# Sums of weights made ahead: seven more pairs a layer with seven products in the down projections of a two-layer mixer kernel

## The chip, the cores and the metric

The kernel runs on one core of a Trainium2 chip. TensorE (PE) multiplies matrices; VectorE (DVE), ScalarE (ACT) and GpSimd (POOL) work on tiles in the on-chip memory, SBUF; PE's results gather in eight banks of PSUM. SyncE (SP) and POOL issue the transfers (DMAs), each through a queue of its own, and 16 DMA engines carry them out. The metric is the device time of one execution in microseconds, the median of several runs. One execution is also taken with the hardware profiler; it has a time of its own, and all durations here come from it.

## The reference, cut to what matters

The model has two layers, on 256 positions of width 2048, in float32. Each layer is a token mixer and a gated MLP with a convolution of width 3:

```python
def conv_ffn(x, w_up, conv_w, conv_b, w_down):
    h = x @ w_up                                  # 256x2048 @ 2048x11008
    C = h.shape[-1]
    h = lax.conv_general_dilated(h, conv_w[:, None, :], ...) + conv_b
    a, g = jnp.split(h, 2, axis=-1)
    return (jax.nn.silu(g) * a) @ w_down          # 256x5504 @ 5504x2048

for i in range(DEPTH):                            # DEPTH = 2
    m = gmlp_mixer(...) if i % 2 == 0 else mla_mixer(...)
    x = layer_norm(ALPHA * x + m, ...)
    x = layer_norm(ALPHA * x + conv_ffn(x, ...), ...)
```

The change concerns `conv_ffn` in both layers: `x @ w_up` is the up projection, `@ w_down` the down projection.

## The kernel before, in words

**Precision.** Each operand of a matmul is split into a high part (a rounded copy, which ACT makes: CAST) and a low part (what the copy lost, which VectorE makes: a subtraction). A product then takes three matmuls: high by high, high by low, low by high. Weights come from memory in float32 as `raw` tiles of 128 x 2048 and are split to `wh` and `wl`.

**Pairs.** The 5504 rows of `w_down` are 43 blocks of 128, taken in 22 pairs (the last holds a single block), and the 2048 columns in two halves of 1024. A pair of blocks with half the columns and the two blocks of 128 positions is a product of 2 by 2 blocks. The eight-product way ("wide") does it in 8 products, 24 matmuls of 128 x 512. The seven-product way is Winograd's: 7 products, 21 matmuls, but it needs sums of weights (`ts`, split to `th` and `tl`) and sums of activations (turned ones, `dn..sx` or `dn..px`) beside the plain parts. Of the plain weights it needs three quarters, 1536 of 2048 columns.

**Kinds.** `PLAN` says for each pair of both halves how it is done: `e` wide; `s` seven with the sums made on the spot by `_seven` (three additions on VectorE, two more splits); `p` parked, a seven whose parts `wh`, `wl`, `th`, `tl` were all made earlier. A layer has 25 `e` (two of them the single block), 10 `s` and 9 `p`.

**Parking.** The parts of the `p` pairs are made while the up projection runs. `park_all` is a generator of small jobs; at set points of the up projection's loop, `next(jobs, None)` takes one. For each pair POOL's queue fetches the weights (`ask`, tile `praw`), one job splits the plain part, the next makes the sums in place (four additions of 512 columns on VectorE) and asks for the next pair, the third splits the sums. The four parts, 3.5 MB a pair, are stored to DRAM through POOL's queue and come back (`fetch`, tiles `fwh`, `fwl`, `fth`, `ftl`) through the same queue a few pairs ahead of their use.

**Order and room.** The feed (class `Feed`) loads and splits ahead of PE by counts: `next()` has two more chunks split than are used and two more loaded beyond these (fewer at a half's end). Tiles are slots of pools: 3 of `raw`, 14 of `big` (the split parts and the activations' parts), 6 of `side` (parked parts). An instruction that writes a tile waits for its slot: SP's next load waits until VectorE has split the chunk that held the slot, and a split waits until PE has used the one that held its tiles. On each engine instructions run in the written order. In the last layer the last four pairs of the last half are kept open and finished together at the end (`late`, skew 4).

**The up projection** takes 86 pieces of `w_up` in groups of four (`gi`), 128 x 2048 each; a piece is split in two halves of 1024 columns. Two groups, 8 and 9, are done as one in pairs instead. Job points are places 1 and 2 of groups 2 to 21, save near that one.

In the trace, `up` is the up projection, `upf` its first group, `dn_q`, `dn_p` and `dn_e` are PSUM banks of the down projection, `xhl` the split input.

Of the kernel before, what the change touches and what calls it, by code (L numbers as in the profile page):

```python
# [8 lines left out]
F32 = mybir.dt.float32  # L9
# [6 lines left out]
P = 128  # L16
# [57 lines left out]
KEEP = {"wide": 4, "seven": 6, "parked": 6}  # L74


def plan(n_k):
# [4 lines left out]
class Feed:  # L82
# [10 lines left out]
    def _load(self):  # L93
        ap, cols, kind = self.chunks[self.loaded][:3]
        if kind == "parked":
            self.fetch(self.loaded)
            self.loaded += 1
            return
        t = self.pool.tile([P, 2048], F32, tag="raw", name=f"raw{self.loaded}", bufs=SLOTS["raw"])
        if len(ap.shape) == 3:  # L100
            self.behind(self.nc.sync.dma_start(t.rearrange("p (k c) -> p k c", k=ap.shape[1]), ap))
        else:
            step = 1024 if self.loaded < 3 else cols
            for o in range(0, cols, step):
                self.behind(self.nc.sync.dma_start(t[:, o : o + step], ap[:, o : o + step]))
        self.raw[self.loaded] = t
        self.loaded += 1

    def _split(self):
        i = self.split  # L110
        cols, kind = self.chunks[i][1:3]
        if kind == "parked":
            self.split += 1
            return
        raw = self.raw.pop(i)
        if kind == "seven":
            self.parts[i] = self._seven(i, raw)
# [18 lines left out]
    def _seven(self, i, raw):  # L136
# [23 lines left out]
    def park(self, i, raw, coming, later):  # L160
# [3 lines left out]
        add = lambda o, a, b: pin(nc.vector.tensor_tensor(o, a, b, ALU.add))  # L164
        self.kept[i] = kept = {}

        def store(n, t, cols):
            d = self.dram.tile([P, cols], F32, tag=f"kept{n}{i}", name=f"kept{n}{i}", bufs=1)
            pin(nc.gpsimd.dma_start(d, t[:, 0:cols].bitcast(F32)))
            kept[n] = d  # L170

        for n, o, cols in (("w", 512, 1536), ("t", 0, 2048)):
            hi, lo = tile(f"p{n}h", F32R), tile(f"p{n}l", F32R)
            pin(nc.scalar.copy(hi[:, 0:cols], raw[:, o : o + cols]))  # L174
            pin(nc.vector.tensor_tensor(lo[:, 0:cols], raw[:, o : o + cols], hi[:, 0:cols].bitcast(F32), ALU.subtract))  # L175
            store(f"{n}h", hi, cols)
            store(f"{n}l", lo, cols)
            if n == "w":
                yield
                r = [raw[:, 512 * i : 512 * (i + 1)] for i in range(4)]  # L180
                add(r[1], r[1], r[0])
                add(r[0], r[0], r[2])
                add(r[2], r[2], r[1])
                add(r[3], r[3], r[2])
                if later is not None:
                    coming.append(self.ask(later))
                yield

    def fetch(self, i):

# [29 lines left out]
def trunk(ctx: ExitStack, tc: tile.TileContext, x, xT, gm_in, gm_wout, ffn_up, ffn_dn,  # L220
# [44 lines left out]
    def back(w, n_k):  # L265

        for hf, units in enumerate(plan(n_k)):
            c = slice(hf * 1024, (hf + 1) * 1024)
            for u, kind in units:
                if 2 * u + 1 == n_k:  # L270
                    chunks.append((w[2 * u, :, c], 1024, kind))
                    continue
                if kind == "parked":
                    parked.append(len(chunks))
                chunks.append((w[2 * u : 2 * u + 2, :, c].rearrange("k p c -> p k c"), 2048, kind))

    def up(layer):

        for gi in range(22):
            if gi - 1 in UP_TOKEN:  # L280
                continue
            if gi not in UP_TOKEN:
                chunks.extend((ffn_up[layer, i], 2048, "") for i in range(4 * gi, min(4 * gi + 4, n_up)))
# [257 lines left out]
    def down(n_k, src, tag, ln, acts, skew=SKEW, tiles=None, beside=None):  # L541
# [6 lines left out]
        for hf, units in enumerate(seq):  # L548
# [3 lines left out]
            for i, (u, kind) in enumerate(units):  # L552
# [11 lines left out]
                if left < skew:  # L564
                    late.append((a, *got))
                elif kind == "wide":
                    acc.eight(a, *got)
                else:
                    acc.seven(a, sums, *got, 512 if kind == "parked" else 0)
# [421 lines left out]
    def ffn(layer, ln, acc, end, last):  # L991
# [75 lines left out]
        for gi in range(1, 22):  # L1067
# [438 lines left out]
```

## Time and profile before

| | us |
|---|---|
| median of 3 runs (lowest, highest) | 2456.43 (2456.2, 2456.98) |
| profiled execution, its own time | 2455.5 |
| its span | 2453.7 |
| PE busy in the span | 2447.7 |
| VectorE busy | 2135.5 |
| ACT busy | 1515.1 |
| up projection of layer 1, from 1972.8 to 2223.0: its main part | 250.2 |
| down projection of layer 1, from 2223.0 to 2444.0 | 221.0 |

How to read it: matmuls are pipelined and their ends are modelled, so a row's mean duration is longer than the distance from one matmul to the next; the pace is a stretch's time by the number of matmuls in it. Line numbers are those of the kernel before; a row names the tile written, the tiles read, the shape and the count. In the views of stretches the columns after the engines' busy times are the granted clock of PE, the DMA engines' share and GB/s.

### The profile page before, as it was taken

What the parts mean: (1) busy time and instruction counts of PE and PEld (TensorE: products, weight loads), DVE (VectorE), ACT (ScalarE), POOL (GpSimd) and SP (SyncE); (2) the same over time, 40 slices, a digit from 0 to 9 for tenths busy, and PEclk for the clock granted to TensorE, in tenths of its full rate; (3) what the DMA queues carried; (4) which work ended last, traced back from release to release, by engine and by line L of the source; (5) the groups of instructions that cost most, each with busy time, mean ns of one, the idle gap of its engine ahead of it and who ended that gap; (6) DMA issues with size and microseconds to landing.
All of it is one profiled execution on the core that took longest, in us unless ns stands there. A gap on an engine that the chain in (4) does not pass through costs nothing. (4 is left out here: it accounts for less than half of the span.)

```text
span 2453.7 us, 32463 instructions
## 1 busy us (share of the span) xinstructions
PE 2447.7 (100%) x12349; PEld 2078.4 (85%) x12349; DVE 2135.5 (87%) x2831; ACT 1515.1 (62%) x2022; POOL 120.4 (5%) x232
## 2 busy tenths in 40 slices
PE   9999999999999999999999999999999999999999
PEld 7888888888888888888888888988888888888887
DVE  7999889989898798988878897868799898878798
ACT  6666777766556666666655466665666666655553
POOL 0000000000000000000001100000001000000100
PEclk9999999999999999999999999999999999999999
DMA  7556665648776687788888985443579687887895
GB/s 293 197 207 214 229 200 192 221 168 308 244 269 245 242 322 287 250 306 335 307 295 321 345 315 178 175 165 122 210 284 341 216 313 305 335 316 274 328 351 195
DMA packets 122508, 639.19 MB, mean 261 GB/s; under 512 B 11096, under 2 KB 11360, under 8 KB 80752
## 3 DMA queue, kind: packets, MB, share of 16 engines
q1 hardware_dynamic: 91632, 460.37, 52.5%
q0 software_dynamic: 30720, 176.75, 19.0%
q8 instruction: 97, 1.59, 0.3%
q14 instruction: 59, 0.48, 0.1%
HBM read 558.38 MB, written 78.69 MB: 260 GB/s over the span
## 5 line engine op out<-in xcount | busy, mean ns | idle before, releaser
L133 DVE TENSOR_TENSOR wl<-raw,wh 128x1024 fp32r<-128x1024 f32 (+4 forms) x625 | 940.5, 1521 | 117.7 <-ACT wh L130 93.3
L130 ACT CAST wh<-raw 128x1024 fp32r<-128x1024 f32 (+4 forms) x625 | 794.1, 1295 | 323.8 <-PE up L240 82.4
L240 PE MATMUL up<-xhl,wh 128*128 128x512 f32 x2368 | 552.2, 390 | 0.0
L240 PEld LDWEIGHTS up<-xhl,wh 128*128 128x128 f32 x2368 | 439.8, 188 | 88.2
L240 PEld LDWEIGHTS up<-xhl,wl 128*128 128x128 f32 x2368 | 294.1, 192 | 5.8
L240 PE MATMUL up<-xhl,wl 128*128 128x256 f32 x2368 | 296.6, 283 | 0.0
L130 ACT CAST th<-ts 128x1536 fp32r<-128x1536 f32 (+1 forms) x172 | 177.4, 1050 | 133.9 <-DVE ts L140 105.0
L133 DVE TENSOR_TENSOR tl<-ts,th 128x1536 fp32r<-128x1536 f32 (+1 forms) x172 | 203.5, 1219 | 20.8 <-PE ub L240 8.2
L240 PE MATMUL ub<-wh,xhl 128*128 128x512 f32 x516 | 161.0, 393 | 0.0
L140 DVE TENSOR_TENSOR ts<-ts,raw 128x512 f32<-128x512 f32 x172 | 118.1, 686 | 1.9
L240 PEld LDWEIGHTS ub<-wh,xhl 128*128 128x128 f32 x516 | 96.9, 188 | 21.8 <-issue 1.9
L140 DVE TENSOR_TENSOR ts<-raw 128x1024 f32<-128x1024 f32 x86 | 104.8, 1218 | 5.1 <-PE ub L240 2.0
L240 PE MATMUL ub<-wl,xhl 128*128 128x512 f32 x258 | 100.5, 389 | 0.0
L240 PE MATMUL v_q<-wh,xhl 128*128 128x512 f32 x224 | 70.7, 391 | 0.0
L240 PE MATMUL v_p<-wh,xhl 128*128 128x512 f32 x192 | 60.0, 389 | 0.0
L240 PEld LDWEIGHTS ub<-wl,xhl 128*128 128x128 f32 x258 | 48.4, 188 | 10.2
L240 PEld LDWEIGHTS v_q<-wh,xhl 128*128 128x128 f32 x224 | 42.0, 188 | 9.9 <-ACT wh L130 1.3
L164 DVE TENSOR_TENSOR praw<-praw 128x512 f32<-128x512 f32 x72 | 49.4, 686 | 0.6
L175 DVE TENSOR_TENSOR ptl<-praw,pth 128x2048 fp32r<-128x2048 f32 x18 | 41.2, 2286 | 3.4 <-ACT pth L174 3.4
L774 ACT ACTIVATE lny<-lnt,lncol 128x128 f32<-128x128 f32 x96 | 36.3, 467 | 12.0 <-PE lnt L770 11.9
L240 PE MATMUL v_q<-wl,xhl 128*128 128x512 f32 x112 | 43.7, 390 | 0.0
L240 PE MATMUL mo<-wh,oT 128*128 128x512 f32 x128 | 42.8, 412 | 0.0
(1910 smaller groups left out, 4656.5 us busy)
## 6 DMA issues: line engine op xcount, KB each, us to landing
raw<-in_ffn_up_dram SPq DMA_DIRECT2D x172, 1024.0 KB, 6.5
raw<-in_gm_in_dram SPq DMA_DIRECT2D x93, 1024.0 KB, 5.4
raw<-in_ffn_dn_dram SPq DMA_DIRECT2D x66, 1024.0 KB, 7.7
raw<-in_gm_wout_dram SPq DMA_DIRECT2D x48, 1024.0 KB, 5.8
praw<-in_ffn_dn_dram POOLq DMA_DIRECT2D x18, 1024.0 KB, 13.7
keptth<-pth POOLq DMA_DIRECT2D x18, 1024.0 KB, 8.2
kepttl<-ptl POOLq DMA_DIRECT2D x18, 1024.0 KB, 9.6
fth<-keptth POOLq DMA_DIRECT2D x18, 1024.0 KB, 9.4
```

Of the source, the lines that this page charges most:

```text
L130: cast = self.nc.scalar.copy(hi, raw)
L133: self.nc.vector.tensor_tensor(lo, raw, hi.bitcast(F32), ALU.subtract)
L140: add = lambda o, a, b: self.nc.vector.tensor_tensor(o, a, b, ALU.add)
L164: add = lambda o, a, b: pin(nc.vector.tensor_tensor(o, a, b, ALU.add))
L175: pin(nc.vector.tensor_tensor(lo[:, 0:cols], raw[:, o : o + cols], hi[:, 0:cols].bitcast(F32), ALU.subtract))
L240: recent[0] = nc.tensor.matmul(o, l, r, start=start, stop=stop, skip_group_check=True)
L774: nc.scalar.activation(y[:, j], t[:, j * P : (j + 1) * P], AF.Identity, bias=lncol[:, o : o + 1], scale=lncol[:, g : g + 1])
```

## The change

A third kind of seven-product pair, `a` ("added"), comes beside the two. Of such a pair only the sums are made ahead: in the up projection POOL's queue fetches the weights, one job makes the four additions in place, and the sums alone, 1 MB in float32, are stored. In the down projection SP loads the three quarters of the plain weights in two DMAs (256 and 512 KB) and the sums in a third (1 MB, tile `rs`, also a `raw` slot), and both are split there (`_added`): two casts on ACT, two subtractions on VectorE, and no tile `ts`.

A layer now has 22 `e`, 7 `s`, 8 `p` and 7 `a`: 22 pairs with seven products, where it had 19. The jobs become steps of their own (`w`, `s`, `t` for a parked pair, `s` alone for an added one), asked for one step ahead, 31 a layer and the first request; `PARK_AT` puts three of them in each of the groups 13, 17 and 18. And pieces of the up projection from group 1 on are split whole, 2048 columns at a time.

```diff
+PARK_AT = {7: (), 10: (3,), 13: (1, 2, 3), 17: (1, 2, 3), 18: (1, 2, 3)}
+AHEAD = 1
...
-        NF_FF: ("0e 1p 2e 3s 4e 5e 6p 7e 8s 9e 10s 11p 12e 13s 14e 15p 16e 17s 18e 19p 20e 21e",
-                "21e 20e 19p 18e 17s 16e 15p 14e 13s 12e 11p 10s 9e 8s 7p 6e 5s 4e 3e 2e 1e 0e")}
-KINDS = {"e": "wide", "s": "seven", "p": "parked"}
+        NF_FF: ("0e 1p 2e 3s 4e 5a 6e 7p 8e 9s 10a 11e 12p 13e 14s 15a 16e 17p 18e 19s 20e 21e",
+                "21e 20p 19e 18a 17e 16s 15p 14e 13a 12s 11e 10p 9e 8a 7s 6e 5p 4a 3e 2e 1e 0e")}
+KINDS = {"e": "wide", "s": "seven", "p": "parked", "a": "added"}
...
-        if len(ap.shape) == 3:
+        if kind == "added":
+            self.behind(self.nc.sync.dma_start(t[:, 512:1024], ap[:, 0, 512:1024]))
+            self.behind(self.nc.sync.dma_start(t[:, 1024:2048], ap[:, 1, :]))
+            s = self.pool.tile([P, 2048], F32, tag="raw", name=f"rs{self.loaded}", bufs=SLOTS["raw"])
+            self.behind(self.nc.sync.dma_start(s, self.kept[self.loaded].pop("s")))
+            t = (t, s)
+        elif len(ap.shape) == 3:
...
-        step = 512 if i == 0 else cols if kind == "wide" and i > 2 else 1024 if cols == 2048 else cols // 2
+        step = 512 if i == 0 else cols if kind in ("wide", "up") and i > 2 else 1024 if cols == 2048 else cols // 2
...
+    def _added(self, i, raw, t):
+        tile = lambda name: self.pool.tile([P, 2048], F32R, tag="big", name=f"{name}{i}", bufs=SLOTS["big"])
+        wh, wl, th, tl = tile("wh"), tile("wl"), tile("th"), tile("tl")
+        self._cast(wh[:, 0:1536], wl[:, 0:1536], raw[:, 512:2048])
+        self.sums = self._cast(th, tl, t)
+        return wh, wl, th, tl
...
+    def steps(self, i):
+        return [(i, n) for n in ("wst" if self.chunks[i][2] == "parked" else "s")]
+
+    def park(self, i, n, raw):
...
+        if n == "s":
+            r = [raw[:, 512 * i : 512 * (i + 1)] for i in range(4)]
+            add(r[1], r[1], r[0])
+            add(r[0], r[0], r[2])
+            add(r[2], r[2], r[1])
+            add(r[3], r[3], r[2])
+            if self.chunks[i][2] == "added":
+                store("s", raw, 2048)
+            return
...
-        coming = [feed.ask(line[0])]
+        steps = [s for i in line for s in feed.steps(i)]
+        asks = [[i for i in line if max(0, steps.index(feed.steps(i)[0]) - AHEAD) == n] for n in range(len(steps))]
+        raws = {i: feed.ask(i) for i in asks[0]}
         yield
-        for i, later in zip(line, line[1:] + [None]):
-            yield from feed.park(i, coming.pop(0), coming, later)
+        for n, (i, s) in enumerate(steps):
+            feed.park(i, s, raws[i])
+            if n + 1 < len(steps):
+                raws.update({i: feed.ask(i) for i in asks[n + 1]})
             yield
...
-                if gi > 1 and gi + 1 not in UP_TOKEN and c in ((3,) if gi - 2 in UP_TOKEN else (1, 2)) and gi + c > 3:
+                if c in PARK_AT.get(gi, (1, 2)) and gi + c > 3:
                     next(jobs, None)
```

How the order of instructions moves, at three places. First SP's queue near the start of layer 1's down projection; the number in a tile's name is that of its chunk (400 is pair 0 of the first half), the one behind it counts tiles. Before:

```order
L101 DMA raw402_19376<-in_ffn_dn_dram 128x2x1024
L101 DMA raw403_19410<-in_ffn_dn_dram 128x2x1024
L101 DMA raw404_19477<-in_ffn_dn_dram 128x2x1024
L101 DMA raw405_19527<-in_ffn_dn_dram 128x2x1024
L101 DMA raw407_19595<-in_ffn_dn_dram 128x2x1024
```

And changed:

```order
L109 DMA raw404_19292<-in_ffn_dn_dram 128x2x1024
L103 DMA raw405_19342<-in_ffn_dn_dram 128x512
L104 DMA raw405_19342<-in_ffn_dn_dram 128x1024
L106 DMA rs405_19345<-kepts405_15754 128x2048
L109 DMA raw406_19375<-in_ffn_dn_dram 128x2x1024
```

Chunk 405, pair 5, was one load and one slot; it is now three loads and two of the three slots, and the load of 406 stands behind them.

The second place is SP's queue at the end of layer 1's second half (439 is pair 4, 443 pair 0). Before:

```order
L101 DMA raw438_20761<-in_ffn_dn_dram 128x2x1024
L669 DMA res3_1_20831<-resd2_1_16428 128x1024 x2
L101 DMA raw439_20793<-in_ffn_dn_dram 128x2x1024
L101 DMA raw440_20848<-in_ffn_dn_dram 128x2x1024
L101 DMA raw441_20878<-in_ffn_dn_dram 128x2x1024
L101 DMA raw442_20914<-in_ffn_dn_dram 128x2x1024
L101 DMA raw443_20916<-in_ffn_dn_dram 128x2x1024
```

And changed:

```order
L103 DMA raw439_20654<-in_ffn_dn_dram 128x512
L104 DMA raw439_20654<-in_ffn_dn_dram 128x1024
L106 DMA rs439_20657<-kepts439_18894 128x2048
L688 DMA res3_1_20702<-resd2_1_16307 128x1024 x2
L109 DMA raw440_20705<-in_ffn_dn_dram 128x2x1024
L109 DMA raw441_20739<-in_ffn_dn_dram 128x2x1024
L109 DMA raw442_20775<-in_ffn_dn_dram 128x2x1024
L109 DMA raw443_20777<-in_ffn_dn_dram 128x2x1024
```

The added pair 439 fills two slots just ahead of the last four loads: 440 takes the third, and 441 and 442 take those that 439 leaves.

The third place is VectorE where layer 1's up projection begins: chunk 319 is a piece of `w_up`, and `xhl3_3` the last quarter of the split input. Before:

```order
L133 TENSOR_TENSOR wl319_15015<-raw319_14988,wh319_15014 128x1024
L778 TENSOR_TENSOR xhl3_3_14793<-lny2_1_3_15007,xhl3_3_14793 128x4x128
L133 TENSOR_TENSOR wl319_15015<-raw319_14988,wh319_15014 128x1024
L133 TENSOR_TENSOR wl320_15059<-raw320_15020,wh320_15058 128x1024 x2
```

And changed:

```order
L141 TENSOR_TENSOR wl319_14942<-raw319_14915,wh319_14941 128x2048
L797 TENSOR_TENSOR xhl3_3_14722<-lny2_1_3_14934,xhl3_3_14722 128x4x128
L141 TENSOR_TENSOR wl320_14984<-raw320_14945,wh320_14983 128x2048
```

The input's last part stood between the two halves of a piece and now stands behind a whole one. On PE, one filler matmul of `up` stood between the first two matmuls of `upf` that read that part; now nine do.

More of the change, by code (lines that the diff above doesn't have):

```diff
@@ L68 @@
                 "23e 22e 21e 20s 19e 18e 17s 16e 15s 14s 13e 12e 11s 10e 9s 8s 7e 6e 5s 4e 3e 2e 1e 0e"),
[L69 to L71 removed]
+        NF_FF: ("0e 1p 2e 3s 4e 5a 6e 7p 8e 9s 10a 11e 12p 13e 14s 15a 16e 17p 18e 19s 20e 21e",
+                "21e 20p 19e 18a 17e 16s 15p 14e 13a 12s 11e 10p 9e 8a 7s 6e 5p 4a 3e 2e 1e 0e")}
+KINDS = {"e": "wide", "s": "seven", "p": "parked", "a": "added"}
 FIRST = ((19, 1), (20, 0), (20, 2))
 LEAD = 5
[L74 removed]
+KEEP = {"wide": 4, "seven": 6, "parked": 6, "added": 6}
 def plan(n_k):
@@ L115, in _split @@
         raw = self.raw.pop(i)
-        if kind == "seven":
-            self.parts[i] = self._seven(i, raw)
+        if kind in ("seven", "added"):
+            self.parts[i] = self._seven(i, raw) if kind == "seven" else self._added(i, *raw)
             self.split += 1
@@ L164, in park @@
         add = lambda o, a, b: pin(nc.vector.tensor_tensor(o, a, b, ALU.add))
-        self.kept[i] = kept = {}
+        kept = self.kept.setdefault(i, {})
         def store(n, t, cols):
             d = self.dram.tile([P, cols], F32, tag=f"kept{n}{i}", name=f"kept{n}{i}", bufs=1)
-            pin(nc.gpsimd.dma_start(d, t[:, 0:cols].bitcast(F32)))
+            pin(nc.gpsimd.dma_start(d, t[:, 0:cols]))
             kept[n] = d
[L172 to L187, printed above, removed]
+        if n == "s":
[7 more added lines that the diff above has]
+            return
+        o, cols = (512, 1536) if n == "w" else (0, 2048)
+        hi, lo = tile(f"p{n}h", F32R), tile(f"p{n}l", F32R)
+        pin(nc.scalar.copy(hi[:, 0:cols], raw[:, o : o + cols]))
+        pin(nc.vector.tensor_tensor(lo[:, 0:cols], raw[:, o : o + cols], hi[:, 0:cols].bitcast(F32), ALU.subtract))
+        store(f"{n}h", hi.bitcast(F32), cols)
+        store(f"{n}l", lo.bitcast(F32), cols)
     def fetch(self, i):
@@ L272, in back @@
                     continue
-                if kind == "parked":
+                if kind in ("parked", "added"):
                     parked.append(len(chunks))
@@ L282, in up @@
             if gi not in UP_TOKEN:
-                chunks.extend((ffn_up[layer, i], 2048, "") for i in range(4 * gi, min(4 * gi + 4, n_up)))
+                chunks.extend((ffn_up[layer, i], 2048, "up" if gi else "") for i in range(4 * gi, min(4 * gi + 4, n_up)))
                 continue
@@ L568, in down @@
                 else:
-                    acc.seven(a, sums, *got, 512 if kind == "parked" else 0)
+                    acc.seven(a, sums, *got, 512 if kind in ("parked", "added") else 0)
                     if u == last:
```

1 line of the change is left out of this document (removed).

## The prediction

> **What bounds the kernel now.** I read the page first, then the chain of waits, the busy times by stage, and last the waits of the engines that feed TensorE.
>
> ```profile
> span 2453.7 us, 32463 instructions
> PE 2447.7 (100%) x12349; PEld 2078.4 (85%) x12349; DVE 2135.5 (87%) x2831; ACT 1515.1 (62%) x2022; POOL 120.4 (5%) x232
> ```
>
> TensorE is busy for all but 2453.7 − 2447.7 = 6.0 us. Since ends of matmuls are modelled, "busy" alone doesn't say that it keeps its pace, so the pace is taken from the chain of waits (start, duration, what):
>
> ```profile
> 1973.06 250.06 PE up L240 x1440
> 2223.12 1.36 PE dn_q L240 x6
> 2438.68 5.46 PE dn_q L240 x24
> ```
>
> Six 512-column matmuls of the down projection in 1.36 us, and 24 in 5.46: 0.227 us each. The last 1440 up matmuls are 45 pieces of 16 matmuls with 512 columns and 16 with 256, 250.06 / 45 = 5.557 us a piece: no piece waited long. The windows give the same by stage, here three up groups, the whole up and down stretch of layer 1, and 20 us in the middle of the down projection:
>
> ```profile
> core 0: us, PE busy (x) PEld busy (x) DVE busy (x) ACT busy (x) POOL busy (x), PEclk, DMA share, GB/s
> 2126.50:2148.70 22.20, 22.20 (x130) 19.66 (x129) 19.21 (x28) 13.89 (x19) 1.09 (x2) 1.00 0.88 334
> 2148.70:2170.90 22.20, 22.20 (x130) 19.66 (x129) 18.82 (x28) 13.35 (x19) 1.06 (x2) 1.00 0.80 297
> 1972.80:2223.00 250.20, 250.20 (x1444) 221.61 (x1443) 210.37 (x304) 156.81 (x223) 18.57 (x33) 1.00 0.82 311
> 2223.00:2444.00 221.00, 221.00 (x977) 183.00 (x976) 192.07 (x259) 111.93 (x118) 16.92 (x32) 1.00 0.81 302
> 2330.00:2350.00 20.00, 20.00 (x90) 16.57 (x89) 19.28 (x26) 9.13 (x9) 1.80 (x4) 1.00 1.01 384
> ```
>
> Down: 221.00 / 977 = 0.226 us a matmul, at a granted clock of 1.00. TensorE's own pace sets the time in both stages, VectorE has 221.0 − 192.1 = 29 us spare in the down stretch and 40 in the up stretch, and the DMA engines are the next nearest resource. So a matmul that goes is worth its 0.2267 us (1.36 / 6) as long as the feeders keep up, and faster feeding alone is worth nothing.
>
> **The change part by part.** *Matmuls.* A wide pair is 24 matmuls, a seven-product pair 21. Per layer 22 instead of 19 pairs have seven products, so 2 × 3 × 3 = 18 matmuls go: 18 × 0.2267 = **−4.08 us**. Nothing else on TensorE is removed or added.
>
> *The feeders in the down projection.* The prices by shape (busy us, mean ns of one):
>
> ```profile
> L133 DVE TENSOR_TENSOR wl<-raw,wh 128x2048 fp32r<-128x2048 f32 x139 | 316.7, 2288 | 62.0 <-ACT wh L130 54.4 <-PE dn_q L240 4.3 <-issue 2.1
> L130 ACT CAST wh<-raw 128x2048 fp32r<-128x2048 f32 x139 | 265.1, 1913 | 90.0 <-DVE tl L133 26.1 <-issue 11.3 <-DMA raw<-in_gm_wout_dram 9.1
> L133 DVE TENSOR_TENSOR tl<-ts,th 128x1536 fp32r<-128x1536 f32 x86 | 150.8, 1754 | 19.7 <-PE ub L240 8.2 <-ACT th L130 5.5 <-PE dn_p L240 2.9
> L133 DVE TENSOR_TENSOR wl<-raw,wh 128x1536 fp32r<-128x1536 f32 x86 | 150.7, 1752 | 8.1 <-PE v_q L240 2.3 <-PE ub L240 2.1 <-ACT wh L130 1.8
> L130 ACT CAST wh<-raw 128x1536 fp32r<-128x1536 f32 x86 | 127.4, 1482 | 72.0 <-DVE tl L133 18.9 <-PE v_q L240 12.9 <-PE ub L240 9.7
> L140 DVE TENSOR_TENSOR ts<-ts,raw 128x512 f32<-128x512 f32 x172 | 118.1, 686 | 1.9
> L140 DVE TENSOR_TENSOR ts<-raw 128x1024 f32<-128x1024 f32 x86 | 104.8, 1218 | 5.1 <-PE ub L240 2.0 <-PE dn_q L240 1.9 <-DMA raw<-in_ffn_dn_dram 0.8
> L133 DVE TENSOR_TENSOR tl<-ts,th 128x512 fp32r<-128x512 f32 x86 | 58.8, 684 | 1.1 <-ACT th L130 1.1
> L130 ACT CAST th<-ts 128x512 fp32r<-128x512 f32 x86 | 53.1, 618 | 23.9 <-DVE ts L140 23.8
> ```
>
> On VectorE a wide pair costs 2.29 us, a seven made on the spot 1.22 + 2 × 0.69 + 1.75 + 1.75 + 0.68 = 6.78, an added pair 1.75 + 2.29 = 4.04, a parked one nothing. Wide go from 25 to 22 a layer, sevens from 10 to 7, parked from 9 to 8, added from 0 to 7: 7 × 4.04 − 3 × 2.29 − 3 × 6.78 = +1.1 us a layer. The turned activations of three more sevens come on top, a few us. ACT gives 7 × (1.48 + 1.91) for 3 × 1.91 + 3 × (1.48 + 1.48 + 0.62): +7.3 us, on an engine with 109 us spare. VectorE's 29 us cover theirs: 0. Without cover each us would cost itself.
>
> *Bytes in the down projection.* A wide or on-the-spot pair loads 1 MB, a parked one fetches 3.5, an added one 0.75 + 1. Per layer 34 + 31.5 = 65.5 MB become 28 + 28 + 12.25 = 68.25 MB, +4.2%: the share of 0.81 becomes about 0.84. Hidden on the mean. The sums leave POOL's queue for SP's, where the added pair issues three loads in place of one, 0.37 us each on a queue that mostly waits for slots:
>
> ```profile
> SPq L101 <- DVE wl L133: 467.9, 94, 12.8
> raw<-in_ffn_dn_dram SPq DMA_DIRECT2D x66, 1024.0 KB, 7.7
> raw<-in_ffn_dn_dram SPq DMA_DIRECT2D x4, 512.0 KB, 5.8
> praw<-in_ffn_dn_dram POOLq DMA_DIRECT2D x18, 1024.0 KB, 13.7
> 2414.06 0.37 SPq L101 DMA_DIRECT2D raw<-in_ffn_dn_dram  x1
> ```
>
> The first row is the wait that the change alters: SP's next load stands until VectorE has split an earlier pair and given its slot back. An added pair takes two of the three slots, so the load behind it is issued only when the pair ahead of it is split. That leaves it about one pair's TensorE time, 24 matmuls or 5.4 us for a wide one, against a median landing of 7.7: 2.3 us later than the pace. What must absorb this is the time by which splits run ahead of their use. In the middle of a half:
>
> ```profile
> 2392.36 2.36 DVE L133 TENSOR_TENSOR tl<-ts,th 128x1536 fp32r<-128x1536 f32 x2
> 2399.53 0.39 PE L240 MATMUL dn_q<-tl,dn18sx 128*128 128x512 f32 x1
> ```
>
> The low sums of pair 8 were ready at 2394.72 and used at 2399.53: 4.8 us ahead. 2.3 fits in that once, and within two or three places of each added pair stands a parked one, which takes no raw slot and gives the loads 21 matmuls, 4.8 us. Bounds per added pair: 0 (absorbed) and 2.3; a gain is excluded, since TensorE had no wait there to lose. I take 0, because 4.8 is twice the deficit.
>
> *The end of the last half.* There the lead is thinnest, and pair 4, just before the last four, becomes an added one:
>
> ```profile
> 2419.92 1.92 ACT L130 CAST wh<-raw 128x2048 fp32r<-128x2048 f32 x1 [1.56 <-DMA raw<-in_ffn_dn_dram]
> 2420.22 4.49 DVE L133 TENSOR_TENSOR wl<-raw,wh 128x2048 fp32r<-128x2048 f32 x2
> 2426.73 0.39 PE L240 MATMUL dn_q<-wl,dn10wx 128*128 128x512 f32 x1
> ```
>
> The last low part is ready at 2424.71 and used at 2426.73: 2.0 us. Its load was issued at 2414.06 and landed at 2419.92, in 5.9 us. At the median of 7.7 it would come 1.8 later and just fit. With the change the loads of pairs 2 and 1 both wait for pair 4's split and then share the engines; the one of pair 0 waits for pair 3's split as before. Bounds: 0, and 2.3, the deficit above with no lead left. I take **+0.4 us**, nearer to 0 since the 2.0 us cover 1.8.
>
> *Up projection: whole pieces.* Two halves cost VectorE 2 × 1.22 and ACT 2 × 1.05, a whole piece 2.29 and 1.91:
>
> ```profile
> L133 DVE TENSOR_TENSOR wl<-raw,wh 128x1024 fp32r<-128x1024 f32 x384 | 459.4, 1218 | 42.3 <-ACT wh L130 34.4 <-issue 5.3 <-PE up L240 1.7
> L130 ACT CAST wh<-raw 128x1024 fp32r<-128x1024 f32 x384 | 389.4, 1052 | 156.3 <-PE up L240 82.4 <-DMA raw<-in_ffn_up_dram 38.5 <-PE dn_q L240 6.9
> ACT wh L130 <- PE up L240: 42.7, 31, 3.2
> ACT wh L130 <- DMA raw<-in_ffn_up_dram: 13.3, 8, 2.8
> ```
>
> 74 pieces × 0.15 and × 0.19: 11 and 14 us less work a layer on engines that aren't the bound: 0. The two wait rows (up stretch of layer 1: total, times, longest) say the same: ACT mostly waits until TensorE frees a tile, so the splits already run as far ahead as the tiles allow. One place pays: where the up projection begins, VectorE's last part of the input's split stands behind a piece.
>
> ```profile
> 1765.21 1.23 DVE L133 TENSOR_TENSOR wl<-raw,wh 128x1024 fp32r<-128x1024 f32 x1 [1.24 <-ACT wh L130]
> 1766.35 0.69 DVE L778 TENSOR_TENSOR xhl<-lny,xhl 128x512 fp32r<-128x512 f32 x1
> 1767.11 0.49 PE L240 MATMUL upf<-wh,xhl 128*128 128x512 f32 x1
> ```
>
> TensorE takes that part at 1767.11, right behind its end at 1767.04. A whole piece ahead of it starts 1.91 − 1.05 later and lasts 2.29 − 1.22 longer: 1.93 us. In the new order TensorE has nine filler matmuls there instead of one, 8 × 0.2267 = 1.81. The rest, 0.1 us in each layer, makes **+0.2**; the bounds are 0 and 2 × 1.93.
>
> *Up projection: jobs.* 28 steps become 32 a layer. A sums step is 4 × 0.69 = 2.74 us of VectorE; fully parked pairs go from 9 to 8, each 2.74 + 1.75 + 2.29 = 6.78:
>
> ```profile
> L164 DVE TENSOR_TENSOR praw<-praw 128x512 f32<-128x512 f32 x72 | 49.4, 686 | 0.6
> L175 DVE TENSOR_TENSOR ptl<-praw,pth 128x2048 fp32r<-128x2048 f32 x18 | 41.2, 2286 | 3.4 <-ACT pth L174 3.4
> L175 DVE TENSOR_TENSOR pwl<-praw,pwh 128x1536 fp32r<-128x1536 f32 x18 | 31.5, 1750 | 0.0
> ```
>
> 7 × 2.74 − 6.78 = +12.4 us, and −11 from the whole pieces: about nothing. POOL's bytes go from 9 × 4.5 = 40.5 MB to 8 × 4.5 + 7 × 2 = 50 a layer, 1.6 MB a job. A group with three jobs moves 4.2 + 5.1 = 9.3 MB (10^6) in 22.2 us, 417 GB/s, against at most 384 seen (at a share of 1.01). Two such groups follow each other: (417 − 384) × 44.4 us = 1.5 MB, a backlog of 3.8 us. Bounds per layer: 0 and 3.8. Two queues share it and ACT's row shows the loads up to 3.2 us early; I take 0.
>
> [...]
>
> **Sum.** −4.08 + 0.4 + 0.2 = −3.5 us on the profiled execution's 2455.5, or 2452.0; the median of the runs is 0.9 above it: 2456.43 − 3.5 = **2452.9 us**. About 0.2%, 4.9 us, is what can be told from no change, so even the bare 4.08 lies inside it.
>
> **Rivals.** *Added pairs starve* (slower): the 2.3 us of lead aren't rebuilt between added pairs, and TensorE stands for them. In full 14 × 2.3 = 32.2: 2456.43 − 4.08 + 32.2 = 2484.6. It decides for slower from (4.08 + 4.9) / 14 = 0.64 us a pair, 2461.3. For it: the slots and the median landing. Against: the 4.8 us of lead, and the parked neighbours. If only what exceeds the thinnest lead, 2.0, counts, 0.3 × 14 = 4.2, it gives 2456.6.
>
> *The backlog shows* (no change): groups 17 and 18 make the up loads late. What passes the 3.2 us is 0.6 a layer; with half of the backlog 1.9 a layer, 2452.9 + 3.8 = 2456.7. For it: 417 against 384. Against: no TensorE wait at 384.
>
> *More than the matmuls* (faster): some of the 6.0 us outside the busy time goes too, where a stage ends with the last pairs or the up projection begins. From 0.8 us on it is over 0.2%: about 2451.2. Against: nothing in the change shortens a boundary.
>
> That the seven-product pairs don't come is excluded by the program: 18 matmuls fewer.
>
> **How the numbers follow.** The forecast, 2451.6 to 2454.5, has 0.62. The backlog, or a thicker end of the last half, 2454.5 to 2457, has 0.16; starved pairs 0.10, of which 0.08 lie above 2461.3; more gain 0.12. Range 2451.2 to 2457.6: it leaves out nearly 0.1 above and some 0.08 below. Faster 0.12, same 0.80, slower 0.08.
>
> **What would show it.** 18 matmuls fewer and a TensorE time per down matmul still 0.227; ACT's waits for raw loads near the added pairs, not passed on to TensorE; the split ahead of the last pair still over zero; ACT waiting for TensorE's tiles in up groups 17 to 19, not for the loads. A down stretch of more than 219 us (221.0 less nine matmuls), or idle TensorE ahead of an added pair's neighbour, makes it wrong; so does a start of the up projection that moves by 1 us.

## The result and the profile after

The changed kernel takes 2489.36 us (median of 4 runs, 2488.5 to 2490.75) against 2456.7 before (4 runs): a ratio of 1.0135, 95% interval 1.0123 to 1.0146. It is 33 us slower, where 3.5 us less was forecast. The profiled execution took 2489.31 us. (Three more pairs a layer have seven products, 22 instead of 19; the seven of the title are the pairs of the added kind.)

The page of the changed kernel, engines and transfers:

```profile
span 2487.4 us, 32347 instructions
PE 2455.7 (99%) x12331; PEld 2076.3 (83%) x12331; DVE 2162.3 (87%) x2757; ACT 1514.9 (61%) x1886; POOL 128.2 (5%) x242
raw<-in_ffn_dn_dram SPq DMA_DIRECT2D x54, 1024.0 KB, 8.0
praw<-in_ffn_dn_dram POOLq DMA_DIRECT2D x30, 1024.0 KB, 13.2
```

The 18 matmuls are gone (12349 to 12331). PE's busy time nevertheless rose by 8 us, and the time outside it from 6.0 to 31.7: PE now waits, and some of its matmuls run slower (12 of them 0.42 us each in the last section's stretch, where the pace is 0.2267). VectorE and ACT have about the same work as before. Where it happens is told by the stretches, in order the second part of layer 0's and of layer 1's up projection, the pair group and the down projection of layer 1 (length, then busy times):

```profile
1018.28:1270.22 251.94, 250.65 (x1444) 221.65 (x1441) 214.85 (x279) 151.14 (x179) 23.13 (x40) 1.00 0.89 338
1991.32:2245.06 253.74, 250.92 (x1443) 221.59 (x1442) 215.10 (x279) 151.23 (x180) 23.12 (x40) 1.00 0.88 335
1941.36:1984.06 42.70, 41.30 (x181) 33.63 (x180) 39.48 (x43) 26.93 (x27) 1.77 (x3) 1.00 0.66 236
2245.06:2477.62 232.56, 224.34 (x967) 182.31 (x966) 202.32 (x275) 121.90 (x127) 14.81 (x28) 0.99 0.82 302
```

| stretch | before | after | without any stall | lost |
|---|---|---|---|---|
| up, pair groups 8 and 9 (both layers) | 40.98 + 40.96 | 42.32 + 42.70 | 81.9 | 3.1 |
| up, groups 10 to 21 (both layers) | 250.14 + 250.14 | 251.94 + 253.74 | 500.3 | 5.4 |
| layer 0, from the first down matmul to a fixed matmul of the MLA's output projection | 426.54 | 438.62 | 424.5 | 14.1 |
| layer 1, down | 221.01 | 232.56 | 219.0 | 13.6 |

("Without any stall" is before less 9 × 0.2267 us in each down projection.) That is 36.2 lost against 4.1 won, 32.1 of the 33.8 us between the two profiled executions; 1.3 more lie in the first 60 us of the program, which the change doesn't touch and which differ by as much between other kernels here.

Who waits for whom, of before in the first row and of after in the others (total us, times, longest):

```profile
ACT wh L130 <- DMA raw<-in_ffn_dn_dram: 8.7, 7, 1.6
```

```profile
ACT wh L138 <- DMA raw<-in_ffn_dn_dram: 53.8, 21, 5.8
ACT pwh L203 <- DMA praw<-in_ffn_dn_dram: 14.4, 2, 8.1
PE dn_q L259 <- DVE wl L141: 9.4, 8, 1.6
PE dn_q L259 <- ACT wh L138: 6.9, 4, 3.0
```

ACT's wait for raw weights of the down projection grew from 8.7 to 53.8 us, and now it reaches PE. The chain of waits around the largest stall of layer 1 (pair 17, behind added pair 18 in the second half; start, duration, what):

```profile
2362.21 2.20 DVE wl L141
2364.41 0.03 DVE dn118at L333
2364.44 10.77 DMA raw<-in_ffn_dn_dram
...
2375.31 1.91 ACT wh L138
...
2377.24 2.30 DVE wl L141
2379.55 0.04 issue
2379.59 2.08 PE dn_q L259 x4
```

The load of pair 17 goes out at 2364.44, the moment VectorE has split pair 19, the one ahead of the added pair: the raw slot is what it waited for. It then takes 10.8 us to land, not the median of 8. PE first waits for the high part, then again for the low part. In the same moments POOL's queue issues:

```profile
2359.15 0.53 POOL L216 DMA_DIRECT2D fwh<-keptwh  x1 [19.17 <-ACT wh L138]
2362.04 0.53 POOL L216 DMA_DIRECT2D fwl<-keptwl  x1 [2.36 <-PE dn_p L259]
2362.57 0.54 POOL L216 DMA_DIRECT2D fth<-keptth  x1
2364.76 0.53 POOL L216 DMA_DIRECT2D ftl<-kepttl  x1 [1.66 <-PE dn_p L259]
```

These are the 3.5 MB of parked pair 15; two of the four DMAs waited until PE had used parts of the parked pair before it. The same chain stands ahead of pair 11 in the first half (issued 2286.07, 10.88 us) and ahead of pair 16 (2312.45, 11.95 us), both right behind added pairs.

At pair 17 something else adds to it: the split of pair 19, which frees the slot, is itself late. ACT has made the high part by 2358.7, and VectorE makes the low part from 2362.14 on:

```profile
2356.80 1.91 ACT L138 CAST wh<-raw 128x2048 fp32r<-128x2048 f32 x1
2362.14 2.28 DVE L141 TENSOR_TENSOR wl<-raw,wh 128x2048 fp32r<-128x2048 f32 x1
```

VectorE isn't idle before it; it works on the results of the first half (`res`, `lnst`) and on turned activations, which stand ahead in its order. So the load waits for VectorE's order at the change of halves too; how much of the stall that makes wasn't tried.

In the up projection it is another transfer. The weights of the parking job in group 18, on ACT and VectorE:

```profile
2184.45 1.48 ACT L203 CAST pwh<-praw 128x1536 fp32r<-128x1536 f32 x1 [8.09 <-DMA praw<-in_ffn_dn_dram]
2186.47 0.48 DVE L1008 SCALAR_TENSOR_TENSOR c_1a<-h_1a,cst,c_1a 128x255 f32<-128x255 f32 x1 [7.37 <-ACT c_1a L1007]
```

ACT stands 8.1 us for weights that were asked for one step earlier, and everything behind it in ACT's order stands too, VectorE among it. The request had gone out at 2169.24 and landed 15.2 us later; the job stood ready 7.1 us after it (2184.45 − 8.09 − 2169.24). In the kernel before, every request went out at least 21.2 us ahead of its job.

### The profile page after: what moved, and what is told of

The parts are those of the page before. It is cut to its first block, busy times and chain, and to the rows that moved or that the text cites. A ratio compares the mean times of both kernels' runs of the same rounds, so it can differ in the third digit from the quotient of the medians.

```text
span 2487.4 us, 32347 instructions
## 1 busy us (share of the span) xinstructions
PE 2455.7 (99%) x12331; PEld 2076.3 (83%) x12331; DVE 2162.3 (87%) x2757; ACT 1514.9 (61%) x1886; POOL 128.2 (5%) x242
## 3 DMA queue, kind: packets, MB, share of 16 engines
q0 software_dynamic: 33696, 189.33, 20.1%
q8 instruction: 97, 1.59, 0.2%
## 5 line engine op out<-in xcount | busy, mean ns | idle before, releaser
L141 DVE TENSOR_TENSOR wl<-raw,wh 128x2048 fp32r<-128x2048 f32 (+4 forms) x479 | 923.3, 1938 | 158.8 <-ACT wh L138 138.9
L138 ACT CAST wh<-raw 128x2048 fp32r<-128x2048 f32 (+4 forms) x479 | 776.3, 1633 | 317.8 <-PE up L259 62.7
L138 ACT CAST th<-ts 128x1536 fp32r<-128x1536 f32 (+1 forms) x160 | 165.8, 1050 | 119.4 <-DVE ts L148 102.0
L141 DVE TENSOR_TENSOR tl<-ts,th 128x1536 fp32r<-128x1536 f32 (+1 forms) x160 | 189.0, 1218 | 12.9 <-PE ub L259 8.2
L148 DVE TENSOR_TENSOR ts<-ts,raw 128x512 f32<-128x512 f32 x160 | 109.8, 686 | 2.0
L148 DVE TENSOR_TENSOR ts<-raw 128x1024 f32<-128x1024 f32 x80 | 97.4, 1217 | 2.2 <-PE ub L259 1.8
L184 DVE TENSOR_TENSOR praw<-praw 128x512 f32<-128x512 f32 x120 | 82.2, 685 | 3.4 <-DMA praw<-in_ffn_dn_dram 2.6
L793 ACT ACTIVATE lny<-lnt,lncol 128x128 f32<-128x128 f32 x96 | 36.3, 466 | 13.8 <-PE lnt L789 13.7
L1024 ACT ACTIVATE s<-c_1g 128x256 f32<-128x256 f32 x43 | 17.9, 417 | 41.7 <-DVE c_1g L1010 41.7
```

What stands on the lines that cost most here:

```text
L138: cast = self.nc.scalar.copy(hi, raw)
L141: self.nc.vector.tensor_tensor(lo, raw, hi.bitcast(F32), ALU.subtract)
L148: add = lambda o, a, b: self.nc.vector.tensor_tensor(o, a, b, ALU.add)
L793: nc.scalar.activation(y[:, j], t[:, j * P : (j + 1) * P], AF.Identity, bias=lncol[:, o : o + 1], scale=lncol[:, g : g + 1])
L1024: nc.scalar.activation(s, cg, AF.Silu)
```

## The experiments

The theory after the result had three parts: (S) the second raw slot of an added pair delays the load behind it; (C) a fetch of a parked pair beside it makes that load long; (R) in the up projection a request one step ahead comes too late where jobs stand three to a group. Rival: the added pairs are simply more work for VectorE and ACT. Each time below stands beside the kernel before on the same chip: 2455.36 (e1 to e4), 2456.5 (e5 to e8), 2456.2 (e9, e10), 2457.8 (e11, e12). All but e10 are single executions. The four of the changed kernel lie within 2.3 us and the six of e10 within 6.4, so smaller differences between whole times show nothing by themselves, and the stretches of the profiles decide.

| run | us | layer 1's down stretch, lost over 219.0 |
|---|---|---|
| changed kernel | 2489.4 | 13.6 |
| e1 sums in a large slot | 2474.0 | 3.6 |
| e2 less fetched | 2478.0 | 5.2 |
| e3 requests two steps ahead | 2491.1 | 17.1 |
| e4 sums on the spot | 2469.1 | 2.6 |
| e5 = e1 + e3 | 2464.1 | 3.3 |
| e6 = e1 + e2 + e3 | 2458.2 | 1.0 |
| e7 three added pairs a layer | 2471.9 | 5.6 |
| e8 whole pieces alone, on the kernel before | 2457.2 | none (221.01, old plan) |
| e9 = e5, job of the pair group moved | 2462.5 | 3.4 |
| e10 = e9, plan mended at two places | 2464.7 | 4.4 |
| e11, e12 = e5, fetch asked later, earlier | 2464.9, 2463.7 | 3.5, 4.1 |

**e1: the slot.**

```diff
-            s = self.pool.tile([P, 2048], F32, tag="raw", name=f"rs{self.loaded}", bufs=SLOTS["raw"])
+            s = self.pool.tile([P, 2048], F32, tag="big", name=f"rs{self.loaded}", bufs=SLOTS["big"])
```

> The sums of an added pair are loaded into a slot of the large pool (14 slots) instead of a second raw slot; all bytes, splits and matmuls stay. Slot theory: the load behind an added pair no longer waits for the split of the pair ahead of it, the stalls behind added pairs go, and the two down projections fall from 230.5 and 232.6 us to about 219 each: some 2465 us in all, 8 us of the up projection remaining. Contention theory (the load lands late because a fetch of 3.5 MB runs beside it): the landings behind added pairs stay near 11 us and the time stays within 5 us of 2489. A third way: the sums now take a large slot early, splits wait for TensorE to free tiles, and it gets no better for that reason.

Measured 2474.0, with the same bytes, splits and jobs. Waits and the down stretch of layer 1:

```profile
ACT wh L138 <- DMA raw<-in_ffn_dn_dram: 5.2, 6, 1.2
ACT pwh L203 <- DMA praw<-in_ffn_dn_dram: 17.7, 2, 10.8
```

```profile
2239.83:2462.38 222.55, 220.00 (x967) 180.91 (x966) 202.09 (x275) 121.80 (x126) 14.83 (x28) 1.00 0.85 315
```

ACT's wait for raw weights falls from 53.8 to 5.2 us, ten of the 13.6 us of layer 1 come back (8.3 of 14.1 in layer 0). VectorE's work is the same 202 us of the stretch, so the rival falls. The 2465 of the slot theory isn't reached: the down projections keep 5.8 and 3.6 us, and the request's wait of the up projection is still there, and longer; layer 0's took 256.5 us with it.

**e2: the bursts.** The fetch loop runs over the two parts of the sums alone, and these stand for the plain parts too.

```diff
-        for n in ("wh", "wl", "th", "tl"):
+        for n in ("th", "tl"):
...
+        got.extend(got[0:2])
```

> Leaves out part of the work: of each parked pair only the two parts of the sums are fetched (2 MB, two slots) and used in place of the plain parts too; the plain parts (1.5 MB) are not fetched. All slots of raw, splits and matmuls stay. Contention theory: the loads behind added pairs land in 6 to 8 us instead of 11 to 12, the down projections fall to 219 to 222 us, 2465 to 2470 in all. Slot theory: the loads are still issued only when the pair ahead is split, so at most the difference in landing is won: some 3 us of 13 in each down projection, about 2483.

Measured 2478.0. The transfers' row of the page, the wait, and the stretch:

```profile
raw<-in_ffn_dn_dram SPq DMA_DIRECT2D x54, 1024.0 KB, 6.5
```

```profile
ACT wh L138 <- DMA raw<-in_ffn_dn_dram: 24.2, 14, 4.5
```

```profile
2242.14:2466.35 224.21, 221.90 (x967) 182.02 (x966) 202.85 (x276) 122.85 (x129) 6.34 (x12) 0.99 0.69 255
```

The median landing falls from 8.0 to 6.5 us, ACT's wait to 24.2, and 8.4 us of the layer's 13.6 are won, where (S) alone allowed some 3. So neither is the cause by itself: the load goes out late and lands late, and taking away either one leaves a stall that the lead can nearly absorb. That the two gains add up to more than the loss (10.0 + 8.4 against 13.6) says the same. The three loads of layer 1 show it one by one (us from issue to landing, and from issue until PE was ready for the pair; between landing and use stand a cast of 1.9 and a subtraction of 2.3 us):

| load of pair | changed: landing, use | e1 | e2 |
|---|---|---|---|
| 11, first half | 10.9, 14.8 | 5.4, 19.4 | 5.7, 15.3 |
| 16, first half | 11.9, 13.7 | 6.7, 20.1 | 5.8, 15.2 |
| 17, second half | 10.8, 10.3 | 6.8, 20.4 | 5.8, 10.3 |

In e2 these loads go out as late as before and land in time. In e1 they go out 5 to 10 us earlier, ahead of the fetch, and so land sooner too; five other loads of the stretch still took 12 to 14 us there, and PE stood for an added pair only at pair 5, 1.6 us, whose own sums took 12.3 us to land. The longest pause that e2 leaves in the layer is at pair 16 of the second half, 2.3 us.

**e3: the request.**

```diff
-AHEAD = 1
+AHEAD = 2
```

> The weights of a parking job are asked for two steps ahead instead of one. If the stalls of the up projection come from a request that lands 15 us late in groups 17 and 18 (ACT stood 8.1 us for it, VectorE behind it), they go: the last stretch of up falls from 251.9 and 253.7 us to about 250.2 each, some 5 us of the whole, and up to 3 us more if the down projection then starts with a larger lead: 2481 to 2485. If the up projection's stalls come from too much work on VectorE, it stays within 1 us of 2489.

```profile
1017.95:1268.10 250.15, 250.15 (x1444) 221.56 (x1442) 216.98 (x280) 152.22 (x180) 22.43 (x39) 1.00 0.89 338
1993.03:2243.17 250.14, 250.14 (x1444) 221.56 (x1441) 216.94 (x280) 152.11 (x180) 22.42 (x39) 1.00 0.88 338
2243.17:2479.20 236.03, 224.59 (x968) 182.12 (x967) 200.88 (x274) 121.65 (x126) 14.85 (x28) 0.99 0.80 295
```

(R) holds for the stage: both stretches are stall-free at 250.15 and 250.14, with all the jobs, with VectorE busy 217 of 250 us and the same 338 GB/s. The whole got no faster, 2491.05, against what was expected: the down projections lost 3.3 and 3.5 us more. In layer 0 slower matmuls account for most of it (see the end): 959 of them kept PE busy for 223.3 us at a mean granted clock of 0.98 (1268.10 to 1501.86), where the changed kernel has 220.7 us and 0.99 for as many (1270.22 to 1500.73), 2.6 us more. In layer 1 the mean clock is 0.99 in both; PE stood 1.8 us at pair 11 of the first half, where it had lost 0.2, and 0.3 to 1.0 us longer at three others. Why isn't settled.

**e4: the same sevens without the added kind.**

```diff
-        NF_FF: ("0e 1p 2e 3s 4e 5a 6e 7p 8e 9s 10a 11e 12p 13e 14s 15a 16e 17p 18e 19s 20e 21e",
-                "21e 20p 19e 18a 17e 16s 15p 14e 13a 12s 11e 10p 9e 8a 7s 6e 5p 4a 3e 2e 1e 0e")}
+        NF_FF: ("0e 1p 2e 3s 4e 5s 6e 7p 8e 9s 10s 11e 12p 13e 14s 15s 16e 17p 18e 19s 20e 21e",
+                "21e 20p 19e 18s 17e 16s 15p 14e 13s 12s 11e 10p 9e 8s 7s 6e 5p 4s 3e 2e 1e 0e")}
```

> The seven added pairs of each layer are made on the spot instead (one load, one raw slot, five large slots, three additions and three splits on VectorE); same matmuls, 22 pairs with seven products; nothing of them is prepared in the up projection. If the slots and bytes of the added kind are the cause: the up projection returns to its old time and the down projections lose their stalls, less what 7 x 2.74 = 19 us more work on VectorE costs (184 + 13 of some 219): between 2452 and 2465. If VectorE's work decides, the down projections stay at 230 or more.

```profile
2231.26:2452.82 221.56, 219.84 (x967) 180.94 (x966) 211.73 (x297) 123.08 (x133) 14.89 (x28) 1.00 0.78 287
```

```profile
PE dn_q L259 <- ACT dn115px L548: 1.7, 1, 1.7
```

2469.1, outside the 2452 to 2465 expected. With nine us more of work on VectorE (211.7 of 221.6, first row) the down projection of layer 1 is nevertheless faster than with added pairs, so it is not that work which stalled the changed kernel. One stall is left in each down projection, at parked pair 15, whose turned activations come late (second row, its wait in layer 1). But VectorE carries its backlog to the end: from the last down matmul to the last of `fin` it takes 9.6 us instead of 5.3. Layer 0's stretch to the output projection lost 8.6.

**e5 and e6: the causes together.** e5 has the edits of e1 and e3, e6 that of e2 as well.

> Sums in a large slot and requests two steps ahead together. If the late request makes the up projection's stalls and the second raw slot most of the down projection's, as two separate causes, they add: up clean at 250.2 us twice, the down projections at 222 us each as with the sums in a large slot alone or a little better, some 2463 us in all. If the up projection only hands its lateness on, the down projections stay longer by what up wins, and it stays at 2474.

> As before, and of each parked pair only the 2 MB of the sums are fetched and used for the plain parts too (leaves 1.5 MB a pair out of the work). If slots, late requests and the fetch bursts are all the causes, no stall is left: down projections of 215.1 and 219.0 us (before, less nine matmuls each), up 250.2, some 2453 us in all. If there is a further cause (VectorE or ACT, the end of the last half), the down projections stay 2 us or more above that.

```profile
2229.94:2452.20 222.26, 219.74 (x968) 180.95 (x967) 200.96 (x274) 121.90 (x126) 14.85 (x28) 1.00 0.85 314
```

```profile
2226.62:2446.61 219.99, 219.44 (x968) 180.97 (x967) 201.28 (x275) 121.63 (x126) 6.34 (x12) 1.00 0.71 258
```

e5 (first row) took 2464.1, as expected from adding the two causes: up clean, and e3's harm in the down projection gone with the slot. In e6 (second row) layer 1 loses 1.0 us and layer 0 1.5 of the 27.7 that the changed kernel lost there: slots, bursts and the late request together account for nearly all of it. What is left: 0.7 us in each down projection at parked pair 15, and 1.5 and 0.8 us in the pair groups, where the stalled matmul waits until VectorE has read the up projection's previous result out of PSUM (`h_0a`), which stands behind splits. In e4 and e8 the pair groups take their old 41.0 us, so it isn't the whole pieces; it changes with the parking jobs, and how isn't settled.

**e7: few added pairs.** The edits of e5, and against the old plan:

```diff
-        NF_FF: ("0e 1p 2e 3s 4e 5e 6p ... 18e 19p 20e 21e",
-                "21e 20e 19p ... 0e")}
+        NF_FF: ("0e 1p 2e 3s 4e 5a 6p ... 18e 19p 20a 21e",
+                "21e 20a 19p ... 0e")}
```

> The old plan with three wide pairs a layer made added ones (5 in the first half, 20 in both): 22 pairs with seven products again, with 9 parked, 10 on the spot and only 3 added; sums in a large slot, requests two steps ahead, whole pieces. The same 18 matmuls are gone. If stalls come with each added pair, 6 instead of 14 leave less than half of them: 2453 to 2457. If they come from the bytes and VectorE's work of 22 sevens in whatever mix, it is 2460 or more.

```profile
1931.48:1977.92 46.44, 43.15 (x182) 34.69 (x180) 42.91 (x49) 27.10 (x28) 0.00 (x0) 0.96 0.51 178
2235.26:2459.82 224.56, 220.82 (x968) 180.86 (x966) 198.67 (x272) 116.88 (x123) 16.98 (x32) 1.00 0.82 308
```

2471.9, above the 2453 to 2457 expected if stalls come with each added pair: three of them lose 5.6 us in layer 1's down stretch, where e5 loses 3.3 with seven, so their number alone is not what counts. Another mix of jobs falls into the pair groups (46.4 us instead of 41.0, VectorE 42.9 busy), and pair 20, added beside a parked one, stalls 3.2 us.

**e8: whole pieces alone,** on the kernel before.

```diff
-        step = 512 if i == 0 else cols if kind == "wide" and i > 2 else 1024 if cols == 2048 else cols // 2
+        step = 512 if i == 0 else cols if kind in ("wide", "up") and i > 2 else 1024 if cols == 2048 else cols // 2
...
-                chunks.extend((ffn_up[layer, i], 2048, "") for i in range(4 * gi, min(4 * gi + 4, n_up)))
+                chunks.extend((ffn_up[layer, i], 2048, "up" if gi else "") for i in range(4 * gi, min(4 * gi + 4, n_up)))
```

> The kernel before with one part of the change alone: pieces of the up projection split whole. By my sum it is worth 0 in the stage and +0.1 us at each start of the up projection: 2455 to 2457 beside the kernel before. If whole pieces delay what stands behind them on VectorE, the pair group of the up projection or its end shows it: over 2458.

```profile
1974.57:2224.71 250.14, 250.14 (x1444) 221.53 (x1441) 208.15 (x261) 153.35 (x181) 18.62 (x33) 1.00 0.82 310
2224.71:2445.72 221.01, 221.01 (x977) 183.00 (x976) 192.14 (x259) 112.09 (x118) 16.96 (x32) 1.00 0.81 302
```

Both stretches as before to 0.01 us; from its first matmul to the pair group each up projection is 0.1 to 0.2 us longer (181.71 to 181.79, 181.87 to 182.03). This part of the change is harmless.

**e9 and e10: towards a version.** Both on e5; e9 has the first edit alone, e10 both.

```diff
-                if c == 0:
-                    next(jobs, None)
...
-        NF_FF: ("0e 1p 2e 3s 4e 5a 6e ...",
-                "21e 20p 19e 18a 17e 16s 15p ...")}
+        NF_FF: ("0e 1p 2e 3s 4e 5s 6e ...",
+                "21e 20p 19s 18a 17e 16e 15p ...")}
```

> Sums in a large slot, requests two steps ahead, and the job inside the pair group of the up projection (groups 8 and 9) left to the next point. If the 1.6 us that TensorE stands in that group comes from a job's tiles, which share slots with that group's turned activations, it goes: 40.98 us there in both layers and about 2462 us in all, the down projections as before at 221 and 222. If it comes from the weights' splits there, it stays and the time is 2464.

> The same, with two more edits in the plan against the two stalls that were left in each down projection: pair 5 of the first half on the spot instead of added (its sums' load landed 15 us late beside a fetch), and in the second half the on-the-spot pair moved from 16 to 19, two pairs away from the parked pair 15 whose turned activations came late; 19 has the same kind in both halves. If these are the causes, the down projections come down to 216 to 217 and 220 us and the kernel to 2453 to 2456, the 4.1 us of the matmuls less 1 to 2. If more work on VectorE for pair 5 or the parked pair's activations still stall it, it stays at 2458 or more.

e9 took 2462.5, but the pair groups still stall (1.6 and 1.5 us; in e5 1.6 in layer 0 alone): the job in them was not the cause. e10 did lose both of the stalls it aimed at, and got a new one ahead of pair 18, 2.4 us, now that an on-the-spot pair stands before it, and 4.6 us in layer 0's pair group: instead of the 2453 to 2456 expected, 1.0030 of the kernel before (1.0017 to 1.0042). No version here beats the kernel before.

**e11 and e12: the fetch asked for at another time.** On e5; e11 as shown, e12 with 7:

```diff
-LEAD = 5
+LEAD = 4
```

> Sums in a large slot, requests two steps ahead, and each parked pair's fetch one pair later (LEAD 4 in place of 5): all work and bytes stay, only the time of the bursts moves by some 5 us against the loads. If the bursts make the loads behind and of added pairs late, the stalls change their places and sizes: the one at pair 5 (1.7 us each layer, its sums landing 15 us after the request beside the fetch of pair 7) goes or falls under 0.5, others may come: 2459 to 2468. If the bursts have no part, the stall at pair 5 stays as it is, with 2464 in all.

> The same with each fetch two pairs earlier (LEAD 7), where the six side slots allow it. If the bursts make the loads late, the stall at pair 5 moves or changes here too; where the slots are still held by the parked pair before, nothing moves (the fetches wait for them in any case): 2460 to 2468. If the bursts have no part, pair 5 stalls by 1.7 us as before and it is 2464.

The stall at pair 5 stayed (1.7 and 1.5 us; 1.8 and 1.7), against the expectation of e11. The rows say why: the request moved, the burst didn't. Of e12, with the fetch asked for earliest:

```profile
2236.60 0.54 POOL L216 DMA_DIRECT2D fwh<-keptwh  x1 [34.59 <-PE dn_p L259]
```

It waits 34.6 us for the side slots of the parked pair before, and goes out 7.7 us after the stretch's first matmul, as in e5 and e11. So these two runs say nothing on (C); e2 and e6 carry it.

## Why the prediction was wrong

**Right.** PE's own pace bounds the kernel before, and 0.2267 us a matmul: where nothing stalls, e3's and e8's stretches stand to 0.01 us. 18 matmuls went. VectorE's and ACT's work was nearly covered (e1; e6 leaves 1.5 and 1.0 us in the down projections), though VectorE's grew by 10 us in layer 1's down stretch, 192.1 to 202.3, where 1.1 and a few were worked out. Whole pieces cost 0.1 to 0.2 us at each start of the up projection, as worked out.

**Wrong: the added pair's price.** The step that failed is "I take 0, because 4.8 is twice the deficit", with the bounds 0 and 2.3 per added pair. The mechanism was named there and made a rival: two of three slots, so the load behind comes one pair late. Three sizes were off.

*The landing.* 7.7 us is a median over loads that differ widely. In layer 1's down stretch of the kernel before:

```profile
DMA to landing us min/median/max: 5.2/7.9/16.2
```

Eight loads took more than 10 us there, most of them issued within 3 us of a fetch, and stalled nothing: they had 23 to 29 us from their issue to their use. The loads behind added pairs that matter here took 10.8 to 12.0, no longer than those, but had 10 to 15. The deficit was 5.3 to 6.5 us, not 2.3.

*The parked neighbours.* The text counts them as relief. They are the burst: a parked pair that has been used frees four slots, and the next one's 3.5 MB start within 3 to 6 us, beside the load that was already late.

*The lead.* 4.8 us was read at a place where nothing took a second slot, and even there it wasn't the thinnest one. In the same stretch a wide pair's low part was ready at 2312.32 and used at 2315.21, 2.9 us ahead:

```profile
2310.03 2.29 DVE L133 TENSOR_TENSOR wl<-raw,wh 128x2048 fp32r<-128x2048 f32 x1 [2.24 <-ACT wh L130]
2315.21 0.39 PE L240 MATMUL dn_q<-wl,dn116wx 128*128 128x512 f32 x1
```

At the added pairs there was less: the low sums of pair 15 of the first half came 2.3 us ahead of their use, those of pair 18, ahead of the largest stall, 0.5.

**Wrong: "Two queues share it and ACT's row shows the loads up to 3.2 us early; I take 0".** The backlog was looked for in the up projection's own loads. It came out in the requests of the jobs, whose landing (13.7 us median, in a row of the prediction) was never set against the time from a request to its job. With three jobs in a group that time shrinks (from 21.2 us at least to 7.1), and a job's cast stands in ACT's fixed order ahead of all that follows. The price was 5.4 us in groups 10 to 21. The bytes themselves were no limit: in e3, group 18 of layer 1 moved more than the 417 GB/s of the sum, and PE kept its pace:

```profile
2170.90:2193.10 22.20, 22.20 (x130) 19.66 (x129) 20.89 (x28) 13.77 (x18) 2.37 (x5) 1.00 1.01 422
```

So 384 GB/s was no ceiling, and the rival "The backlog shows" isn't what happened.

**No term at all: the pair groups.** They lost 3.1 us; the sum of the jobs looks at groups 17 and 18 alone.

**The end of the last half,** taken at 0.4, cost 1.0 at pair 0 and 0.7 at pair 4.

**The rivals.** "Added pairs starve" is what happened, with 2484.6 us in full against 2489.4 measured, of which 27.7 us are in the down projections where it had 32.2. The agreement is partly luck: not every added pair stalled, few did and by more, and slow matmuls stood behind some of the pauses (12 at 0.42 us behind the largest of layer 1). It was given a chance of 0.10 because the lead of 4.8 us and the parked neighbours were counted against it.

## What to carry to other kernels

Where a load waits for a slot, price it by when it can go out and by what else is in flight at that moment, not by the median landing: set the time from its issue to its use against the longest landings that the trace already shows, and look up the neighbours' bursts and what releases them. This kernel, at PE's pace with leads of 2.0 to 4.8 us, had no room for a kind of work that takes two of three slots: it saved 2.0 us of matmuls in layer 1's down stretch and lost 13.6; count slots before instructions. And when jobs are packed more densely, set each one's transfer time against the time between its request and its use: here one late tile stopped ACT for 8.1 us, and VectorE behind it for 7.4.

## What the runs showed of the hardware

Pauses of PE cost more than their length here where the granted clock dropped after them. In the stall of the chain above, with pauses of 2.37 and 1.59 us, it falls to half (length, busy times, granted clock third from the end):

```profile
2377.00:2379.80 2.80, 0.94 (x3) 0.51 (x4) 2.56 (x3) 1.28 (x4) 0.00 (x0) 0.69 0.69 281
2379.80:2384.80 5.00, 5.00 (x12) 3.92 (x13) 5.00 (x7) 3.43 (x3) 0.53 (x1) 0.50 0.55 184
2384.80:2390.00 5.20, 5.20 (x24) 4.25 (x23) 3.89 (x6) 3.15 (x3) 0.00 (x0) 0.99 0.90 323
```

12 matmuls in 5 us, 0.42 each, and then 24 in 5.2 again: 5.0 − 12 × 0.2267 = 2.3 us lost on top of the pauses. That is part of why PE's busy time grew by 8 us with fewer matmuls. In e1 the clock dropped after a single pause of 1.59 us:

```profile
1305.95 0.50 PE L259 MATMUL dn_q<-tl,dn05ax 128*128 128x512 f32 x1 [1.59 <-DVE tl L141]
```

```profile
1306.60:1309.70 3.10, 3.10 (x9) 2.41 (x8) 3.03 (x6) 0.77 (x2) 0.00 (x0) 0.52 0.00 1
```

Nine matmuls of the 3.1 us from 1306.60 on ran at a clock of 0.52. The pause of 1.59 us that ends at 2328.77 in the changed kernel had no such wake: the clock is 1.00 from 2328.80 to 2333.00, with 18 matmuls in 4.2 us. What decides it wasn't tried.

The DMA engines moved 422 GB/s for this one core over a whole group of 22.2 us (e3, above), and 416 over 3 us at a share of 1.03 (2374.0 to 2377.0 of the changed kernel):

```profile
2374.00:2377.00 3.00, 0.89 (x4) 0.39 (x3) 0.00 (x0) 1.69 (x1) 0.00 (x0) 1.00 1.03 416
```
